# Seven block products for gate and up in layer 0 as in layer 1, activation forms summed by accumulating DMAs, and adaLN columns spread anew, in a two-layer trunk

## The chip, the cores and the metric

The kernel runs as one program on one core of a Trainium2 chip. The metric is the time of one execution on the device, in microseconds. TensorE does the matmuls, ScalarE (ACT) and VectorE (DVE) the elementwise work, GpSimd (POOL) some sums; SyncE (SP) and GpSimd issue the DMAs.

## The reference, cut to what matters

Two layers work on x of 512 tokens by 1024 channels, in float32. Each layer has a mixer and a gated MLP of inner width 2816. The adaLN parameters are six vectors of 1024 for each layer, from one conditioning vector. The change touches the MLP of layer 0, the forms of both MLPs, and the time at which adaLN columns are computed.

```python
def adaln_params(c, w, b):
    m = jax.nn.silu(c) @ w + b
    return [t[:, None, :] for t in jnp.split(m, 6, axis=-1)]

def conv_ffn(h, w_gate, w_up, conv_w, conv_b, w_down):
    a = causal_dwconv(h @ w_gate, conv_w, conv_b)
    return (jax.nn.silu(a) * (h @ w_up)) @ w_down

for layer in range(DEPTH):
    sh1, sc1, g1, sh2, sc2, g2 = adaln_params(c, ada_w[layer], ada_b[layer])
    h = rms_norm(x, norm_mix_g[layer]) * (1.0 + sc1) + sh1
    ...
    x = x + g1 * mix
    h = rms_norm(x, norm_ffn_g[layer]) * (1.0 + sc2) + sh2
    x = x + g2 * conv_ffn(h, ffn_w_gate[layer], ffn_w_up[layer], ffn_conv_w[layer],
                          ffn_conv_b[layer], ffn_w_down[layer])
```

## The kernel before, in words

Activations are kept transposed: 128 channels on the partitions, 512 tokens along the row, and 8 such chunks for 1024 channels. Every projection is a product of three matmuls (`mm3`, L209): each operand is split into a rounded high part and a remainder, and high by high, high by low and low by high are added up in PSUM. A weight unit is 128 x 1024 (512 KB). SyncE loads it, ScalarE writes its high part (`whi`, L169 or L200), VectorE the remainder (`wlo`, L170 or L201). The tokens form two halves of 256, LO and HI.

**The MLP in layer 0** (`ffn`, L705) takes the 22 blocks of 128 inner channels one after the other. For each, gate and up are 24 matmuls of 512 columns each. The blocks come in groups of 8, 7 and 7; after a group the down projection of that group runs for 8 output chunks m, and `add_x` (L324) adds each to x. The first two blocks are done by `ffn_start` (L690), half by half, while the norm of the other half is still being written. After each block `ada_step(3)` (L229) handles three adaLN columns: a load of 512 KB and one VectorE operation (L225). Behind the last down projection `tail` (L630) lets the next layer's norm begin, and `kv_start` (L1042) starts the K and V projections of layer 1; `prefetch` and `take` (L183, L188) prepare weights ahead in the order of `unit_order`.

**The MLP in layer 1** (`ffn_pairs`, L771) takes the first two blocks in the same way, and the other 20 as ten pairs. For a pair, gate and up together are a 2 x 2 product of blocks (gate and up by channels 0 to 511 and 512 to 1023, times LO and HI tokens), and seven products A to G take the place of eight (`product`, L906). Each product has 2 x 12 matmuls of 256 columns. Four of the products use sums of weights: s1 and s3 are added up by accumulating DMAs of GpSimd (L868), s2 and s4 by GpSimd's tensor operation (L873). Four use sums of activations, the forms n1, n2, t3 and t4: GpSimd first adds high and low parts (`whole`, L811), VectorE subtracts (`form`, L819 and L821), and ScalarE and VectorE split the result.

The order of a pair stage is set by the list `order`: product A of pair i, then B, C, D of pair i - 1, then E, F, G of pair i. After pairs 3 and 7 a down phase of 8 chunks is put in. `upkeep` (L1003) runs ahead of the list: it loads up to 9 entries ahead, starts up to 4 sums, and prepares up to 4 weights. Buffers come from rings: 3 for "raw" tiles, 4 for "sw" (sums and D's weight), 2 for "adaw" (s2 and s4), 4 for prepared weights.

## Time and profile before

| | before |
|---|---|
| time of three runs | 1144.04, 1148.44, 1151.24 us (median 1148.44) |
| the profiled execution | 1145.14 us |
| its span on the core | 1143.4 us |
| TensorE busy | 1112.9 us, 97% |
| VectorE busy | 834.5 us, 73% |
| ScalarE busy | 535.4 us, 47% |
| GpSimd busy | 111.2 us, 10% |

The span is the time from the first to the last instruction of the profiled execution; 1.7 us lie around it. "Busy" is the time in which an engine executes. TensorE's matmuls overlap one another, so its cost is read from the distance of their starts and not from their durations.

### The profile page before, as it was taken

How to read it: one execution, taken by the hardware profiler on the slowest of the kernel's cores; microseconds unless marked ns; L12 is line 12 of the kernel's file. 1: busy time of each engine (PE TensorE's matmuls, PEld its weight loads, DVE VectorE, ACT ScalarE, POOL GpSimd, SP SyncE). 2: the span in 40 equal slices, each digit the busy share in tenths (PEclk: the TensorE clock that was granted, in tenths of full speed). 3: DMA queues.
4: the chain of work that ended last, by engine and by line, in shares of the span. 5: the costliest groups of instructions: out<-in, count | busy, mean ns of one | idle time of the engine just before them, and what ended most of it. 6: DMA issues, size and time to landing. Idle time of an engine off the chain costs nothing.

```text
span 1143.4 us, 16343 instructions
## 1 busy us (share of the span) xinstructions
PE 1112.9 (97%) x6290; PEld 937.4 (82%) x6290; DVE 834.5 (73%) x1283; ACT 535.4 (47%) x864; POOL 111.2 (10%) x99
## 2 busy tenths in 40 slices
PE   8998998999999999999999999999899999999998
PEld 7866776798878888888889766678899889998997
DVE  6975899888873587456557578967999539974873
ACT  4465778354331333223335466644566326641550
POOL 0010000000000000000000111211633102411200
PEclk9999899999999999999999999999999999999999
DMA  9879573625874477445241421035358527573521
GB/s 341 297 188 234 179 213 121 199 69 168 274 225 143 135 225 236 160 148 164 81 143 57 111 57 55 19 93 143 80 136 222 158 77 198 135 236 92 132 72 74
DMA packets 49147, 174.03 MB, mean 152 GB/s; under 512 B 5583, under 2 KB 6735, under 8 KB 48367
## 3 DMA queue, kind: packets, MB, share of 16 engines
q1 hardware_dynamic: 44830, 156.64, 42.9%
q0 software_dynamic: 4240, 16.35, 7.8%
q8 instruction: 49, 0.80, 0.3%
q14 instruction: 28, 0.23, 0.1%
HBM read 164.06 MB, written 2.10 MB: 145 GB/s over the span
## 4 chain that ended last, share of the span: by engine, by line
PE 80%; DVE 9%; DMA 4%; ACT 3%; issue 2%; POOL 1%; SPq 0%; DVEq 0%; ACTq 0%; POOLq 0%
PE y L917 9%; PE d L212 7%; PE d L211 7%; PE d L210 7%; PE x L917 7%; DMA adaw<-adaw 4%; PE g L210 3%; PE g L212 3%; PE g L211 3%; PE u L212 3%; PE u L210 3%; PE u L211 3%; PE o L210 2%; PE o L212 2%; PE o L211 2%
## 5 line engine op out<-in xcount | busy, mean ns | idle before, releaser
L169 ACT ACTIVATE whi_w<-raw_w 128x1024 fp32r<-128x1024 f32 (+1 forms) x113 | 117.8, 1043 | 187.6 <-PE d L211 80.0
L170 DVE TENSOR_TENSOR wlo_w<-raw_w,whi_w 128x1024 fp32r<-128x1024 f32 (+1 forms) x113 | 135.9, 1203 | 46.0 <-ACT whi_w L169 43.5
L225 DVE CUSTOM_DVE_ANT_0 adaw<-adaw,c_s,col 128x1024 f32<-128x1024 f32 x80 | 101.3, 1279 | 35.1 <-DMA adaw<-adaw 34.9
L324 DVE SCALAR_TENSOR_TENSOR x<-d,ada,x 128x512 f32<-128x512 f32 (+1 forms) x51 | 36.6, 719 | 113.9 <-PE d L212 113.9
L211 PE MATMUL g<-h,whi_w 128*128 128x512 f32 (+1 forms) x192 | 72.2, 376 | 3.5 <-DVE h L301 3.5
L210 PE MATMUL g<-h,whi_w 128*128 128x512 f32 (+1 forms) x192 | 72.4, 377 | 1.6 <-ACT h L299 1.4
L212 PE MATMUL u<-h,wlo_w 128*128 128x512 f32 (+1 forms) x192 | 72.1, 376 | 0.0
L210 PE MATMUL d<-ah,whi_w 128*128 128x512 f32 (+1 forms) x190 | 71.9, 378 | 0.2 <-ACT ah L200 0.2
L210 PE MATMUL u<-h,whi_w 128*128 128x512 f32 (+1 forms) x192 | 72.0, 375 | 0.0
L212 PE MATMUL g<-h,wlo_w 128*128 128x512 f32 (+1 forms) x192 | 72.0, 375 | 0.0
L211 PE MATMUL d<-al,whi_w 128*128 128x512 f32 (+1 forms) x190 | 70.8, 373 | 0.8 <-DVE al L201 0.8
L211 PE MATMUL u<-h,whi_w 128*128 128x512 f32 (+1 forms) x192 | 71.5, 372 | 0.0
L212 PE MATMUL d<-ah,wlo_w 128*128 128x512 f32 (+1 forms) x190 | 71.3, 376 | 0.0
L873 POOL TENSOR_TENSOR r_s<-r_s,r_a 128x1024 f32<-128x1024 f32 x20 | 55.1, 2755 | 147.6 <-DVE wlo_s L201 50.2
L200 ACT ACTIVATE whi_s<-r_s 128x1024 fp32r<-128x1024 f32 x40 | 42.5, 1062 | 46.0 <-PE d L211 17.8
L212 PE MATMUL d<-ah,wlo_d 128*128 128x512 f32 (+1 forms) x158 | 60.8, 385 | 0.0
L210 PE MATMUL d<-ah,whi_d 128*128 128x512 f32 (+1 forms) x158 | 60.1, 380 | 0.6 <-DVE x L324 0.6
L211 PE MATMUL d<-al,whi_d 128*128 128x512 f32 (+1 forms) x158 | 60.5, 383 | 0.0
L917 PE MATMUL y<-h,whi_a 128*128 128x256 f32 x320 | 57.1, 280 | 1.0 <-DVE gt L789 1.0
L1121 POOL COPY sc<-nsink 128x4 f32<-128x4 f32 x16 | 3.4, 217 | 560.9 <-PE d L212 502.3
L917 PE MATMUL y<-forms,whi_s 128*128 128x256 f32 x320 | 56.6, 279 | 0.1
L201 DVE TENSOR_TENSOR wlo_s<-r_s,whi_s 128x1024 fp32r<-128x1024 f32 x40 | 51.9, 1297 | 5.6 <-ACT whi_s L200 4.7
(332 smaller groups left out, 3119.8 us busy)
## 6 DMA issues: line engine op xcount, KB each, us to landing
raw_w<-wu SPq DMA_DIRECT2D x104, 512.0 KB, 3.8
adaw<-adaw SPq DMA_DIRECT2D x80, 512.0 KB, 4.4
r_a<-ws SPq DMA_DIRECT2D x30, 512.0 KB, 3.8
r_s<-ws SPq DMA_DIRECT2D x20, 512.0 KB, 4.6
r_s<-ws POOLq DMA_DIRECT2D x20, 512.0 KB, 7.2
first_w<-adaw SPq DMA_DIRECT2D x16, 512.0 KB, 5.7
r_d<-wu SPq DMA_DIRECT2D x16, 512.0 KB, 5.2
raw_w<-w SPq DMA_DIRECT2D x16, 448.0 KB, 3.4
```

The source lines that it names most:

```text
L169: pin(A.activation(hi[:, :n], raw[:, :n], AF.Copy))
L170: pin(V.tensor_tensor(out=lo[:, :n], in0=raw[:, :n], in1=hi[:, :n].bitcast(F32), op=ALU.subtract))
L200: A.activation(dst_hi, src, AF.Copy)
L201: V.tensor_tensor(out=dst_lo, in0=src, in1=dst_hi.bitcast(F32), op=ALU.subtract)
L210: PE.matmul(out, whi, rhi, start=first, stop=False)
L211: PE.matmul(out, whi, rlo, start=False, stop=False)
L212: return PE.matmul(out, wlo, rhi, start=False, stop=last)
L225: return V.tensor_tensor_reduce(out=t, in0=t, in1=c_s, scale=1.0, scalar=C(f"ada_b{l}", s * 8 + m), op0=ALU.mult, op1=ALU.add, accum_out=a ...
L324: V.scalar_tensor_tensor(out=x[:, m, sl], in0=bank[:, sl], scalar=ada_ap(l, s, m), in1=x[:, m, sl], op0=ALU.mult, op1=ALU.add)
L873: G.tensor_tensor(out=self.t, in0=self.base[0].t, in1=self.base[1].t, op=ALU.add)
L917: m = [PE.matmul(out, w[a][:, o:o + P], b[c][:, k], start=slot in "AEF" and k + a + c == 0, stop=k == 3 and a == 1, skip_group_check=True) ...
L1121: nc.gpsimd.tensor_copy(sc[:, :, 256:257], nsink[:, 4 * kv:4 * kv + 4].unsqueeze(2))
```

## The change

One function `ffn` now serves both layers, and both take gate and up of the ten pairs as seven block products. In layer 0 this puts 1680 matmuls of 256 columns in the place of 960 of 512 columns. The groups of 8, 7 and 7 are gone; the down projection runs after pairs 3 and 7 and in pieces at the end, as layer 1 did.

The forms of both layers are made in another way. While a norm's chunk is written, ScalarE writes a second output from the same input (`extra`): b11 and n21 in the LO half, n12 and b22 in the HI half, which are whole activations with a plus or a minus. GpSimd then adds them by accumulating DMAs from SBUF to SBUF (`add_to`), of 256 KB each, and ScalarE and VectorE split the sums. The tensor operations L811, L819 and L821 are gone.

The adaLN columns become entries of the list `order` (`ada_item`) and load into the ring "sw", which grows from 4 to 6 buffers. In layer 0 one stands in each of the stages 2 to 9, two ahead of each of the 16 down blocks, and two near the end. 53 columns are left when the MLP of layer 0 begins, before and after the change; 42 are now handled in it, 3 at the end of layer 1's attention, and 8 around the first down phase of layer 1.

The rest of the lists: `upkeep` looks 12 entries ahead for loads instead of 9; the activations of the inner blocks have 8 buffers for each of the two names instead of 10; at the end of layer 0 the weights of V and of the last two down blocks are prepared, then `prefetch(1)` prepares one more, and `tail` begins. The gate weights of the recurrence move to a tile with two buffers.

```diff
+        nrm.forms = b = b_forms(l)
+        def extra(m, sl, t):
+            if m < 4:
+                A.activation(b["b11"][:, m], t[:, sl], AF.Identity, bias=ada_ap(l, 3, m))
+            else:
+                A.activation(b["n21"][:, m - 4], t[:, sl], AF.Identity, bias=nsh[:, l, m:m + 1], scale=-1.0)
+        nrm.extra = extra
         for u in range(2):
...
+    def ffn(l, nrm, nxt=None, before=None, after=None):
         LO, HI = HALVES
...
+            early = [bank(n == "u", f"{n}{l}_{i}") for i in range(2) for n in ("g", "u")]
+            units = [unit(f"{n}{l}", i) for i in range(2) for n in ("g", "u")]
+            pairs = [(b, take(u, 2 - j, pin)) for j, (b, u) in enumerate(zip(early, units))]
+            proj2(pairs, LO)
+            b11, n21 = (nrm.forms[n] for n in ("b11", "n21"))
+            n12, b22 = act_tiles(f"n12_{l}", (P, 2, 256), F32), act_tiles(f"b22_{l}", (P, 2, 256), F32)
+            def extra(m, sl, t):
+                if m < 4:
+                    A.activation(n12[m // 2][:, m % 2], t[:, sl], AF.Identity, bias=nsh[:, l, m:m + 1], scale=-1.0)
+                else:
+                    A.activation(b22[m // 2 - 2][:, m % 2], t[:, sl], AF.Identity, bias=ada_ap(l, 3, m))
+            nrm.extra = extra
+            nrm.start(HI)
+            nrm.half(HI)
+            rings = {"raw": (3, []), "sw": (6, []), "adaw": (2, []), "w": (4, [])}
...
+            def add_to(a, b):
+                for i in range(2):
+                    G.dma_start(a[i], b[i], accum_op=ALU.add)
+            def split_form(dst, src, neg=False):
+                for i in range(2):
+                    hi, lo = (d[:, 2 * i:2 * i + 2] for d in dst)
+                    A.activation(hi, src[i], AF.Copy, scale=-1.0 if neg else 1.0)
+                    if neg:
+                        V.scalar_tensor_tensor(out=lo, in0=src[i], scalar=-1.0, in1=hi.bitcast(F32), op0=ALU.mult, op1=ALU.subtract)
+                    else:
+                        V.tensor_tensor(out=lo, in0=src[i], in1=hi.bitcast(F32), op=ALU.subtract)
+            def twos(t):
+                return [t[:, 2 * i:2 * i + 2] for i in range(2)]
+            fb, fn = twos(b11), twos(n21)
+            def first_form():
+                add_to(fb, n12)
+                split_form(n1, fb)
+            def other_forms():
+                b, n = fb, fn
+                add_to(b, b22)
+                split_form(n2, b, True)
+                add_to(b22, n12)
+                add_to(b, n)
+                split_form(t3, b22)
+                split_form(t4, b)
             st = [{} for _ in range(NST)]
...
             def slot(i, n):
                 order.append((blocks[i][n], lambda w: product(i, n), True))
 
-            tails = [Item(f"dt{i}", ws[4 * NST + i], "raw") for i in range(3)]
+            def ada_item():
+                if ada_q:
+                    q = ada_q.pop(0)
+                    order.append((Item("ada_%d_%d_%d" % q, adaw[q[0], q[1] * 8 + q[2]], "sw", ada=q), None, True))
+            tails = [Item(f"dt{l}_{i}", ws[l * NWS + 4 * NST + i], "raw") for i in range(3)]
             for i in range(NST):
                 slot(i, "A")
                 if i:
                     for n in "BCD":
                         slot(i - 1, n)
+                if l == 0 and i > 1:
+                    ada_item()
                 for n in "EFG":
                     slot(i, n)
                 if i in DOWN_AFTER:
                     gi = DOWN_AFTER.index(i)
                     for m in range(KC):
-                        order.append((Item(f"d{gi}_{m}", wu[UNITS["d1"] + 8 * gi + m], "raw"),
+                        ada_item()
+                        ada_item()
+                        order.append((Item(f"d{l}_{gi}_{m}", wu[UNITS[f"d{l}"] + 8 * gi + m], "raw"),
                                       lambda w, gi=gi, m=m: down(gi, m, w), True))
             order.append((tails[0], lambda w: down_part(0, w), False))
             slot(NST - 1, "B")
@@ -996,13 +972,17 @@
             slot(NST - 1, "C")
             slot(NST - 1, "D")
             order.append((tails[1], lambda w: (down_part(2, w), down_part(3, w)), True))
+            ada_item()
+            ada_item()
             order.append((tails[2], down_rest, True))
...
+            def upkeep(c, sums=4):
+                for it, _, _ in order[c:c + 12]:
                     if it.t is None and it.base is None:
                         if not it.room():
...
+            rings["w"][1].extend(Held() for _ in range(2))
+            upkeep(0, 2)
+            first_form()
+            for i in ((0, 1), (2, 3)):
+                proj2([pairs[j] for j in i], HI)
+            n2, t3 = (pair_of(t) for t in kept(f"forms{l}", [P, 2, 4, 256]))
+            forms = {"A": p11, "B": t3, "C": p22, "D": t4, "E": p21, "F": n1, "G": n2}
+            other_forms()
+            for held in rings["w"][1][:2]:
+                held.left = 0
+            for f in range(2):
+                finish(f, early[2 * f], early[2 * f + 1], 1.0)()
+            for c, (it, run, done) in enumerate(order):
                 upkeep(c)
+                if it.ada is not None:
+                    with tc.high_priority(offset=-100):
+                        pin(ada_col(*it.ada, it.t))
+                    it.left = 0
+                    continue
...
+                return None
+            pending.extend(unit_order(1))
+            prep_spare([unit("l1_v", u) for u in range(2)], kept("spare1", [P, 2, 1024]))
+            for it in last[2:]:
+                it.prep()
+            prefetch(1)
+            tail(nxt, lambda m, sl, mid=None: down_last(m, last[m - 4].w, (sl,), mid), (KC - 2, KC - 1), before)
+            return after()
 
```

What this does to the order of the instructions is seen at three places.

ScalarE, second half of the norm at the start of layer 0's MLP: `h` are the high parts that gate and up of the first two blocks wait for, `ahn` and `aln` are n12, `ahb` and `alb` b22, `b` is b11, `n` is n1. Before:

```order
L299 ACTIVATE h_0_1880<-ht_1_3_256_2280,ada 128x256 [waits DVE_49]
L299 ACTIVATE h_0_1880<-ht_1_4_256_2284,ada 128x256 [waits DVE_49]
L299 ACTIVATE h_0_1880<-ht_1_5_256_2288,ada 128x256 [waits DVE_49]
L299 ACTIVATE h_0_1880<-ht_1_6_256_2292,ada 128x256 [waits DVE_49]
L299 ACTIVATE h_0_1880<-ht_1_7_256_2296,ada 128x256 [waits DVE_49]
L169 ACTIVATE whi_w_2448<-raw_w_2446 128x1024 [waits DMAHW6_49,PE_49]
```

After:

```order
L296 ACTIVATE h_0_1880<-ht_1_4_256_2301,ada 128x256 [waits DVE_49]
L748 ACTIVATE ahb_0_2271<-ht_1_4_256_2301,ada 128x256
L296 ACTIVATE h_0_1880<-ht_1_5_256_2306,ada 128x256 [waits DVE_49]
L748 ACTIVATE ahb_0_2271<-ht_1_5_256_2306,ada 128x256
L841 ACTIVATE n_0_2321<-b_0_1886 128x512 [waits DMASW5_49,Activation_49]
L296 ACTIVATE h_0_1880<-ht_1_6_256_2311,ada 128x256 [waits DVE_49]
L748 ACTIVATE alb_0_2272<-ht_1_6_256_2311,ada 128x256
L296 ACTIVATE h_0_1880<-ht_1_7_256_2316,ada 128x256 [waits DVE_49]
L748 ACTIVATE alb_0_2272<-ht_1_7_256_2316,ada 128x256
L841 ACTIVATE n_0_2321<-b_0_1886 128x512 [waits DMASW6_49,Activation_49]
```

The extra outputs stand between the high parts, and the first split of n1 stands ahead of the chunks 6 and 7 with a wait for an accumulating DMA.

VectorE, end of a down phase (`x<-d` are the last output chunks, `wlo` the remainders of the weights of the next products). Before, in layer 1:

```order
L324 SCALAR_TENSOR_TENSOR x<-d_0_5_7964,ada,x 128x512 [waits PE_49]
L201 TENSOR_TENSOR wlo_s_3_7991<-r_s_3_7888,whi_s_3_7990 128x1024 [waits DMASW6_49,Activation_49]
L324 SCALAR_TENSOR_TENSOR x<-d_0_6_7994,ada,x 128x512 [waits PE_49]
L201 TENSOR_TENSOR wlo_s_3_8023<-r_s_3_7650,whi_s_3_8022 128x1024 [waits Activation_49]
L324 SCALAR_TENSOR_TENSOR x<-d_0_7_8026,ada,x 128x512 [waits PE_49]
L201 TENSOR_TENSOR wlo_a_3_8055<-r_a_3_7890,whi_a_3_8054 128x1024 [waits Activation_49]
L201 TENSOR_TENSOR wlo_a_4_8089<-r_a_4_7923,whi_a_4_8088 128x1024 [waits DMAHW6_49,PE_49,Activation_49]
```

After, in layer 0, the same place:

```order
L322 SCALAR_TENSOR_TENSOR x<-d_0_5_3592,ada,x 128x512 [waits PE_49]
L322 SCALAR_TENSOR_TENSOR x<-d_0_6_3633,ada,x 128x512 [waits PE_49]
L197 TENSOR_TENSOR wlo_s_0_3_3619<-r_s_0_3_3586,whi_s_0_3_3618 128x1024 [waits DMASW2_49,Activation_49]
L197 TENSOR_TENSOR wlo_s_0_3_3662<-r_s_0_3_3248,whi_s_0_3_3661 128x1024 [waits Activation_49]
L221 ISA r_ada_0_1_3510,ada<-r_ada_0_1_3510,c_s,col 128x1024 [waits DMAHW4_49]
L221 ISA ada 128x1
L221 ISA r_ada_0_2_3513,ada<-r_ada_0_2_3513,c_s,col 128x1024 [waits DMAHW5_49]
L221 ISA ada 128x1
L221 ISA r_ada_0_3_3548,ada<-r_ada_0_3_3548,c_s,col 128x1024 [waits DMAHW7_49]
L221 ISA ada 128x1
L322 SCALAR_TENSOR_TENSOR x<-d_0_7_3669,ada,x 128x512 [waits PE_49]
L197 TENSOR_TENSOR wlo_a_0_3_3698<-r_a_0_3_3590,whi_a_0_3_3697 128x1024 [waits DMAHW2_49,Activation_49]
```

The adaLN columns (L221) now stand between the last chunks and the remainders.

TensorE, the first matmuls of K and V for layer 1 behind the down projection (`k_0`, `k_1` are K's two banks, `v_0` a bank of V, `h_0` and `h_1` high and low parts of the norm). Before:

```order
L210 MATMUL k_0_4871<-h_0_1880,whi_w_4689 128x256 [waits Activation_49]
L211 MATMUL k_0_4871<-h_1_1881,whi_w_4689 128x256 [waits DVE_49]
L212 MATMUL k_0_4871<-h_0_1880,wlo_w_4690 128x256
L210 MATMUL k_1_4872<-h_0_1880,whi_w_4721 128x256
L211 MATMUL k_1_4872<-h_1_1881,whi_w_4721 128x256
L212 MATMUL k_1_4872<-h_0_1880,wlo_w_4722 128x256
L210 MATMUL k_0_4871<-h_0_1880,whi_w_4689 128x256 [waits Activation_49]
L211 MATMUL k_0_4871<-h_1_1881,whi_w_4689 128x256 [waits DVE_49]
L212 MATMUL k_0_4871<-h_0_1880,wlo_w_4690 128x256
L210 MATMUL k_1_4872<-h_0_1880,whi_w_4721 128x256
```

After, from the sixth chunk of the same half on:

```order
L206 MATMUL k_0_5930<-h_0_1880,whi_5792 128x256 [waits Activation_49]
L207 MATMUL k_0_5930<-h_1_1881,whi_5792 128x256 [waits DVE_49]
L208 MATMUL k_0_5930<-h_0_1880,wlo_5793 128x256
L206 MATMUL k_0_5930<-h_0_1880,whi_5792 128x256 [waits Activation_49]
L207 MATMUL k_0_5930<-h_1_1881,whi_5792 128x256 [waits DVE_49]
L208 MATMUL k_0_5930<-h_0_1880,wlo_5793 128x256
L272 MATMUL ms_0_256_6044<-ones,acc_0_1879 128x1 [waits DVE_49]
L272 MATMUL ms_0_256_6044<-ones,acc_0_1879 128x1
L206 MATMUL k_1_5931<-h_0_1880,whi_5938 128x256 [waits Activation_49]
L207 MATMUL k_1_5931<-h_1_1881,whi_5938 128x256
L206 MATMUL v_0_5932<-spare_0_5768,h_0_1880 128x256
```

Before, the products of `k_1` are interleaved with those of `k_0`; after, they follow behind the whole half of `k_0`, with a wait for ScalarE, and `ms` of the other half's norm stands ahead of them.

## Rows read from the trace of the kernel before

**Rows 1.** The page: the busy times, the chain's shares by engine
```profile
PE 1112.9 (97%) x6290; PEld 937.4 (82%) x6290; DVE 834.5 (73%) x1283; ACT 535.4 (47%) x864; POOL 111.2 (10%) x99
...
PE 80%; DVE 9%; DMA 4%; ACT 3%; issue 2%; POOL 1%; SPq 0%; DVEq 0%; ACTq 0%; POOLq 0%
```

**Rows 2.** Windows: stretch and length, then busy time by engine, granted clock, DMA share, GB/s
```profile
241.80:608.70 366.90, 365.87 (x1738) 305.77 (x1739) 239.88 (x336) 125.49 (x166) 0.00 (x0) 1.00 0.53 168
608.70:632.40 23.70, 23.70 (x203) 23.62 (x201) 19.76 (x42) 11.83 (x22) 0.33 (x2) 1.00 0.23 67
800.00:840.00 40.00, 34.60 (x254) 33.15 (x254) 38.18 (x50) 21.88 (x36) 23.50 (x12) 0.91 0.41 98
836.00:838.00 2.00, 2.00 (x12) 2.00 (x10) 2.00 (x4) 0.52 (x2) 0.38 (x1) 0.51 0.77 203
860.00:880.00 20.00, 20.00 (x172) 20.00 (x172) 19.38 (x22) 12.57 (x18) 6.75 (x4) 1.00 0.71 187
901.00:938.00 37.00, 37.00 (x163) 30.36 (x162) 15.52 (x14) 7.44 (x7) 3.99 (x2) 1.00 0.30 95
962.00:982.00 20.00, 20.00 (x179) 20.00 (x178) 18.88 (x22) 13.11 (x19) 6.50 (x4) 1.00 0.65 171
```

**Rows 3.** The chain (start, us, what): direct matmuls in layer 0, products in layer 1
```profile
265.59 0.23 PE g L210
...
377.06 0.23 PE g L210
...
388.04 0.23 PE g L210
...
861.76 2.83 PE x L917 x24
...
966.84 2.72 PE y L917 x24
```

**Rows 4.** Waits of TensorE, 785 to 842 us: us in total, times, longest
```profile
PE g L211 <- DVE h L301: 3.5, 4, 1.6
...
PE y L917 <- DVE gt L789: 1.0, 1, 1.0
PE y L917 <- DVE wlo_a L201: 1.0, 1, 1.0
```

**Rows 5.** Timeline of VectorE: start, us, line, operation, tiles, count, idle time before
```profile
613.96 0.89 DVE L301 SCALAR_TENSOR_TENSOR h<-ht,ada,h 128x256 fp32r<-128x256 f32 x2 [0.19 <-ACT h L299]
...
801.61 3.53 DVE L301 SCALAR_TENSOR_TENSOR h<-ht,ada,h 128x256 fp32r<-128x256 f32 x2 [0.18 <-ACT h L299]
...
960.25 3.84 DVE L201 TENSOR_TENSOR wlo_a<-r_a,whi_a 128x1024 fp32r<-128x1024 f32 x2
...
965.18 1.22 DVE L201 TENSOR_TENSOR wlo_s<-r_s,whi_s 128x1024 fp32r<-128x1024 f32 x1 [0.42 <-ACT whi_s L200]
```

**Rows 6.** The page, DMA issues: KB each, median us from issue to landing
```profile
adaw<-adaw SPq DMA_DIRECT2D x80, 512.0 KB, 4.4
...
r_s<-ws POOLq DMA_DIRECT2D x20, 512.0 KB, 7.2
...
k<-k POOLq DMA_DIRECT2D x4, 256.0 KB, 4.7
```

**Rows 7.** The page, costliest groups: the adaLN operation
```profile
L225 DVE CUSTOM_DVE_ANT_0 adaw<-adaw,c_s,col 128x1024 f32<-128x1024 f32 x80 | 101.3, 1279 | 35.1 <-DMA adaw<-adaw 34.9
```

**Rows 8.** Groups of VectorE and GpSimd at the forms of layer 1
```profile
L819 DVE SCALAR_TENSOR_TENSOR r<-r,r 128x512 f32<-128x512 f32 x4 | 4.8, 1230 | 0.0
L821 DVE TENSOR_TENSOR r<-r,r 128x512 f32<-128x512 f32 x4 | 3.2, 813 | 1.1 <-POOL r L811 1.1
...
L811 POOL TENSOR_TENSOR r<-h,h 128x512 f32<-128x512 f32 x8 | 12.1, 1527 | 39.1 <-DVE h L301 39.1
```

**Rows 9.** Waits of TensorE, 80 to 135 us
```profile
PE gr L210 <- ACT ge L529: 4.1, 1, 4.1
PE pr L210 <- ACT xcs L200: 2.2, 1, 2.2
```

More of the change, by code (lines that the diff above doesn't have):

```diff
@@ L792, in finish @@
                 return close
-            def pair_of(t):
-                return [t[:, i] for i in range(2)]
-            n1 = pair_of(pool.tile([P, 2, 4, 256], F32R, tag="n1", name="n1", bufs=1))
-            n2, t3 = (pair_of(t) for t in kept("forms", [P, 2, 4, 256]))
-            half = [slice(0, 4), slice(4, 8)]
-            b11, b21 = ([h[:, k, LO] for h in (hh, hl)] for k in half)
-            b22 = [h[:, half[1], HI] for h in (hh, hl)]
-            t4 = [h[:, half[0], HI] for h in (hh, hl)]
@@ L888, in ffn_pairs, with __init__ @@
             class Held:
-                def __init__(self, item):
-                    item.held, self.left = self, 1
+                def __init__(self, item=None):
+                    self.left = 1
+                    if item is not None:
+                        item.held = self
             blocks = []
             for i in range(NST):
-                b = [ws[4 * i + j] for j in range(4)]
-                a11, a12 = Item(f"a11_{i}", b[0], "raw"), Item(f"a12_{i}", b[1], "raw")
-                a22 = Item(f"a22_{i}", b[3], "sw")
@@ L899, in ffn_pairs @@
[L899 to L903 removed]
+                b = [ws[l * NWS + 4 * i + j] for j in range(4)]
+                a11, a12 = Item(f"a11_{l}_{i}", b[0], "raw"), Item(f"a12_{l}_{i}", b[1], "raw")
```

285 lines of the change are left out of this document (97 added, 188 removed).

## The prediction

> **What bounds the kernel now.** The page comes first: TensorE is busy for 97% of the span and holds 80% of the chain of waits, the next engine is VectorE with 73% [rows 1]. So time can only go if TensorE gets less to do, or less to wait for, and each edit is priced by what TensorE issues and by what it is made to wait for. Then the windows, stage by stage. Layer 0's MLP lasts 366.9 us, TensorE idles for 1.0 us of them, VectorE works 239.9 (65%), GpSimd not at all [rows 2]: this stage is bound by matmuls alone. In layer 1 the stages of pairs look different: TensorE is full there too, but VectorE works 18.9 to 19.4 us of every 20 [rows 2]. The one place in layer 1's MLP where TensorE waits is its beginning: of the 40 us from 800 on it is busy for 34.6, at a granted clock of 0.91 [rows 2], and its waits name VectorE: 3.5 us for the norm's second half, 1.0 for a weight's remainder, 1.0 for the first inner block [rows 4].
>
> **The change part by part.** All sums are made against the profiled execution of 1145.1 us; the median of the runs is 1148.4, 3.3 above it, and the change in us is then taken from the median.
>
> *The products.* A direct matmul of 512 columns costs TensorE (388.04 - 377.06)/48 = 0.229 us [rows 3]; 960 of them are 219.6 us. The products have two prices in layer 1: 2.83 us for 24 before the first down phase, 2.72 behind it [rows 3]. Four stages of seven slots at the first and six at the second are 79.2 + 114.2 = 193.5. That is **-26.1**. If the higher price held in all ten stages, it would be 4.6 less. The down projection keeps its 528 matmuls' worth of columns and is taken at the same price. The 1.0 us of waiting [rows 2] is replaced by what follows: **-1.0**.
>
> *The beginning of layer 0's MLP.* Now the 192 matmuls of the first two blocks run from 241.8 to 265.6, 23.8 us [rows 2, 3]. In the new order ScalarE meets the first split of n1 ahead of the last two chunks, and this waits for an accumulating DMA from SBUF to SBUF of 256 KB. No such DMA is in the trace. The nearest are GpSimd's plain ones of that size, 4.7 us, and its accumulating ones of twice the size, 7.2 [rows 6]. The last two chunks come some five chunks behind the output that the DMA adds; at about 1 us for a chunk, and near 1 us for the issue (my estimate, from the 6 us that the eight chunks at the start of K and V take, below), the wait is between 0.7 and 3.2, and with the added outputs on ScalarE I take 2.7. TensorE needs these chunks at once, so nothing hides it. Next, t4 stands at the end of a chain of three such additions, 14.1 to 21.6 us from the first. VectorE has t4's split ahead of the remainder for A of the second pair; from the first addition TensorE has about 4 us of the second half and four products of 2.83 to do, 15.3 us of cover. The wait is then 0 to 6.3; I take 2.2, nearer to the plain DMA since the size is its size. The two waits of layer 1 that follow on a VectorE that is behind, 1.0 and 1.0 [rows 4], I take over: 2.0. Together **+6.9**, between 1 and 13.
>
> By the Trainium skill (DMA: Bandwidth & Descriptors, the section on the anatomy of one DMA on the GpSimd path) a DMA costs about 2.0 us plus its bytes at 436 GB/s, 2.6 us for 256 KB, an estimate from its figures; the row of that size shows 4.7. By the page's figure the waits for both splits would go and the sum would be about 4 us lower.
>
> *adaLN columns in the stages.* One is 1.28 us on VectorE [rows 7] and a read of 0.08. A stage of 19.04 us holds 18.88/20 of VectorE's time, 18.0 us, in the undisturbed window [rows 2]; with a column it is 19.3, over by 0.3. That is 2.4 us over eight stages, if nothing else gives way; VectorE's small idle pieces say less, a column meeting a sum on GpSimd says more: two remainders took 3.84 us there where one alone takes 1.22 [rows 5], so 1.4 us for one encounter. At the two passages from a down phase to the next stage, three columns (4.1 us) stand on VectorE between the last chunks' residuals and the remainders for D and A, as the order shows; one column each is taken to show on TensorE, 2.6 us. Sum **+5.0**, between 0 and 14. In the down phases themselves 16 columns are 21.8 us, beside 15.52/37 x 44 = 18.5 of work [rows 2], 40.3 of 44 us: covered, by little. Their loads raise 95 GB/s by 16 x 0.52 MB in 44 us, 191, to 286 GB/s; the row's 0.30 for 95 GB/s makes that a share of 0.90 [rows 2]. Covered too, but a load can be late, and SyncE issues the columns' loads ahead of weights; a cost is left to a rival. The eight columns in layer 1's down phase find 21 idle us [rows 2], and the three at the end of its attention lie beside the output projection: 0 for both, at most 4.1 for the latter.
>
> *The start of K and V.* In the trace TensorE is full from 608.7 to 632.4 [rows 2], because two weights of K and a part of V feed on every chunk that comes. The last of the eight chunks is done at 614.85 [rows 5]. In these 6.15 us it does 52 matmuls of 0.118 (2.83/24). With only k_0 at hand it can do 24; the other 28 are late: 3.3 us. k_1's high part stands behind the last chunk on ScalarE, its remainder on VectorE; half a remainder, 0.6, is added. And a TensorE that is fed in pieces is granted a lower clock: after two waits of 1.0 [rows 4] the window from 836 to 838 shows 0.51, the lower level of 1.2 GHz, and 12 matmuls where 17 belong [rows 2]; 0.7 for that. **+4.6**, between 3 and 8.
>
> *The forms in layer 1.* VectorE loses 4.8 + 3.2 us of subtractions, and GpSimd 12.1 us of sums [rows 8]. What VectorE then has left over goes into the 2.0 us of waits behind the second half [rows 4] and the 1 us that the low clock cost [rows 2]: all but 1 us of the 3. The 3.5 us in the second half [rows 4] I leave, since in the new order the split of n1 waits in that place, and n12's DMAs stand behind two weight sums and two weight DMAs on GpSimd. **-2.0**, between -6 and +2.
>
> What was slow about the old forms shows in one row: two operations of the norm took 3.53 us on VectorE while GpSimd added [rows 5], the same pair at the start of K and V 0.89. The Trainium skill (SBUF — State Buffer, the section on who interferes with whom) has a rule for this: a VectorE instruction with two inputs from SBUF contends with a GpSimd instruction that reads SBUF, and a DMA contends with no compute engine. By it the 3.5 us go too; the same rule speaks against layer 0, which gets 20 more sums of weights on GpSimd.
>
> *The recurrence.* The gates' weights and loads move a little; TensorE waits there for 4.1 and 2.2 us [rows 9], for ScalarE, whose order changes only in two splits. Zero, between -2 and +2.
>
> Sum: -26.1 - 1.0 + 6.9 + 5.0 + 4.6 - 2.0 = **-12.6**: 1132.5 for the profiled execution, 1135.8 for the median, **1136**.
>
> **The rivals.**
>
> *The gain arrives nearly whole.* The additions land in time and VectorE keeps up. For it speaks that VectorE has 35% of layer 0's MLP free [rows 2]. The Trainium skill's rule on contention (SBUF — State Buffer, above) speaks for it in layer 1 as well. Left are -27.1, the late 28 matmuls (+3.3), and -5 in layer 1: -28.8, 1120.
>
> *Layer 0 becomes bound by VectorE and the loads.* VectorE has 0.3 us too much in every stage with a column, and the queues run at 0.90 in the down phases, so that a late weight stops TensorE. The upper ends hold: +14 for the +5.0, and 3 more at the beginning: -0.6, 1148, no change. Against it: the ring of prepared weights is four deep, and the stages of layer 1 at 18.9 of 20 show no wait on TensorE.
>
> *Slower than before.* One mechanism: the chain of additions. My 2.2 us for t4 stand for (15.3 + 2.2)/3 = 5.8 us an addition. Each further us costs three in each layer, six in all. At 8.0 us nothing is left of the gain; at 10, which a queue shared with weight DMAs of 7.2 [rows 6] could give, it is 1136 + 25 = 1161.
>
> That the products stay at 2.83 in all of layer 0 gives 1140; it lies inside the forecast's own range.
>
> **How the numbers follow.** The forecast, 1127 to 1142, gets 0.45; the whole gain (1115 to 1127) 0.22; the bound layer 0 (1142 to 1154) 0.27; the chain 0.06. A measurement of this kernel can tell about 1%, 11.5 us, from no change: faster is under 1137, slower over 1160. Some three quarters of the forecast lie under 1137 with the whole gain: 0.56 faster, 0.38 the same, 0.06 slower. The range leaves out a third of the whole gain at the bottom, and the chain and the upper end of the third case at the top: 1118 to 1150.
>
> **What would show it.** The products: some 193 us between the first A and the last D of layer 0, without the down blocks, and 24 in 2.72 to 2.83. The beginning: the wide part starts 26 to 27 us behind the first matmul, and the largest waits name the split of n1 and a remainder. The columns: VectorE over 18.5 of 19 us in stages 4 to 9, and waits of TensorE for remainders behind the down phases. K and V: 24 matmuls in the first 6 us, and a granted clock under 1. Layer 1: waits of 3 to 4 us in the second half, and no low clock behind it. The prediction fails if the additions land much earlier or later than 5.8 us, or if VectorE's overload adds up over the stages.

## The result and the profile after

The changed kernel takes 1178.42 us (median of four runs, 1175.28 to 1180.48), the kernel before 1147.56 beside it (1144.04 to 1151.24). The ratio is 1.0266 with a 95% interval from 1.0226 to 1.0307: slower by 2.7%, about 31 us. The forecast was 1136 with a range up to 1150; the result lies outside it, on the other side.

The profiled execution after took 1175.28 us with a span of 1173.5, 30.1 more than before. The page's busy times answer to [rows 1]:

```profile
PE 1106.1 (94%) x7004; PEld 967.9 (82%) x7004; DVE 905.2 (77%) x1374; ACT 596.7 (51%) x973; POOL 174.8 (15%) x147
```

TensorE's busy time fell by 6.8 us, its idle time rose from 30.5 to 67.4. So less work was bought with more waiting. Where it waits is found by cutting the span at five starts of TensorE that both traces have: the first gate matmul of layer 0's MLP, the first K matmul behind it, the first gate matmul of layer 1's MLP, the first pair product of layer 1, and the last matmul, which starts 3.9 and 3.8 us ahead of the span's end.

| stretch | before, us | after, us | difference | forecast |
|---|---|---|---|---|
| up to layer 0's MLP (the recurrence) | 241.8 | 245.8 | +4.0 | 0 |
| layer 0's MLP | 367.0 | 376.7 | +9.7 | -15.2 |
| K, V and the attention of layer 1 | 180.9 | 185.0 | +4.1 | +4.6 |
| start of layer 1's MLP, to its first product | 30.9 | 39.6 | +8.7 | 0 |
| the rest, to the last matmul | 318.9 | 322.6 | +3.7 | -2.0 |

The -2.0 of the forecast stands in the last row because the two waits that it counts on, for `gt` and `wlo_a` [rows 4], lie behind layer 1's first product, which starts at 820.6 us in the kernel before. Two places hold most of the miss: layer 0's MLP, 25 us worse than forecast, and the start of layer 1's MLP, 8.7 worse. The windows of the trace after show both (stretch and length, then busy time of TensorE, its weight loads, VectorE, ScalarE and GpSimd, granted clock, DMA share, GB/s; they answer to [rows 2]):

```profile
245.80:622.50 376.70, 353.67 (x2453) 330.37 (x2453) 312.76 (x407) 177.09 (x256) 74.28 (x48) 0.96 0.69 200
260.00:280.00 20.00, 17.18 (x123) 16.97 (x124) 15.63 (x20) 10.39 (x19) 11.82 (x11) 0.83 0.98 210
345.00:392.00 47.00, 47.00 (x224) 39.28 (x224) 34.23 (x50) 10.51 (x12) 0.88 (x1) 1.00 0.76 246
392.70:433.50 40.80, 32.46 (x241) 31.59 (x240) 32.13 (x39) 16.54 (x23) 13.67 (x8) 0.87 0.77 207
409.40:416.50 7.10, 5.35 (x24) 5.05 (x25) 7.05 (x7) 3.95 (x5) 5.46 (x3) 0.52 0.47 107
440.00:460.00 20.00, 20.00 (x172) 20.00 (x171) 19.96 (x24) 12.59 (x18) 6.76 (x4) 1.00 0.70 208
528.50:569.10 40.60, 32.57 (x241) 31.80 (x240) 32.70 (x40) 16.54 (x23) 13.72 (x8) 0.87 0.73 209
622.50:628.70 6.20, 4.34 (x21) 2.73 (x19) 5.65 (x15) 2.98 (x8) 0.32 (x2) 1.00 0.00 0
807.50:847.10 39.60, 27.70 (x201) 26.52 (x202) 23.14 (x40) 17.93 (x39) 15.08 (x13) 0.87 0.83 206
```

Read these against each other. In a stage of pairs (440 to 460) VectorE has no time left, 19.96 of 20, and TensorE is full all the same. In the first down phase (348.8 to 392.7; the window is 345 to 392) TensorE is full too, and the DMA share is 0.76. But each passage from a down phase to the next stage (392.7 to 433.5 and 528.5 to 569.1) holds ten products, which at the paces of [rows 3] are 27.2 to 28.3 us, and takes 40.7. This is where layer 0 lost its gain: 25 to 27 us in two places, at a granted clock of 0.87.

What TensorE waits for in the first passage (waits of TensorE, 385 to 435 us: total, times, longest):

```profile
PE y L878 <- DVE x L893: 3.9, 1, 3.9
PE x L878 <- ACT whi_s L196: 2.6, 1, 2.6
PE x L878 <- DVE wlo_s L197: 1.7, 1, 1.7
```

`whi_s` and `wlo_s` are the split sums of weights. The waits make 8.2 us of the 12.5 to 13.6; the rest goes with the low clock that follows on them: the 24 matmuls of the window from 409.4 to 416.5 take 5.35 us at a granted clock of 0.52, near the lower level of 1.2 GHz, in place of 2.83. ScalarE's row says what the split waited for, and the timeline of SyncE's queue says why that came late (start, us, line, operation, tiles):

```profile
408.32 1.06 ACT L196 ACTIVATE whi_s<-r_s 128x1024 fp32r<-128x1024 f32 x1 [11.45 <-DMA r_s<-ws]
```

```profile
373.07 0.33 SPq L781 DMA_DIRECT2D r_a<-ws  x1
374.28 1.54 SPq L781 DMA_DIRECT2D r_ada<-adaw  x2
379.77 0.33 SPq L781 DMA_DIRECT2D r_s<-ws  x1
380.98 0.33 SPq L781 DMA_DIRECT2D r_a<-ws  x1
391.84 0.33 SPq L781 DMA_DIRECT2D r_ada<-adaw  x1
394.18 1.53 SPq L781 DMA_DIRECT2D r_s<-ws  x2
396.59 0.33 SPq L781 DMA_DIRECT2D r_a<-ws  x1
```

`r_s` are the weights that the next stage adds up, `r_ada` the adaLN columns. From 318 to 375 SyncE issued 16 columns and not one `r_s`; between 380.98 and 391.84 it issued nothing at all; and the weights of the sum for the product that was due at 406.8 were loaded at 394, with the addition still to come (it landed at 408.2). Columns and sums share the ring "sw". The longest wait, for `x`, is VectorE's: it came to that operation late, behind a remainder of 2.79 us that ran beside another late sum on GpSimd.

At the start of layer 1's MLP GpSimd stands in the way, and ScalarE behind it (timelines of the two engines):

```profile
810.42 1.84 POOL L789 DMA_DIRECT2D r_s<-ws  x2 [38.12 <-DVE ht L292]
819.48 5.03 POOL L794 TENSOR_TENSOR r_s<-r_s,r_a 128x1024 f32<-128x1024 f32 x2 [7.22 <-DVE ht L292]
824.47 1.74 POOL L789 DMA_DIRECT2D r_s<-ws  x2
825.59 1.51 POOL L836 DMA_DIRECT2D b<-ahn  x1
```

```profile
826.40 0.51 ACT L296 ACTIVATE h<-ht,ada 128x256 fp32r<-128x256 f32 x1
826.81 0.49 ACT L748 ACTIVATE ahb<-ht,ada 128x256 f32<-128x256 f32 x1
836.75 0.63 ACT L841 ACTIVATE n<-b 128x512 fp32r<-128x512 f32 x1 [9.44 <-DMA b<-ahn]
837.29 0.49 ACT L296 ACTIVATE h<-ht,ada 128x256 fp32r<-128x256 f32 x1
```

The addition `b<-ahn` (n12 into b11) is issued behind two sums and four accumulating weight DMAs and lands 11.1 us later; ScalarE's split of n1 waits 9.44 us for it, and the chunk of the norm that TensorE needs (`h` at 837.29) stands behind the split. TensorE's wait for that chunk is the 9.3 here (waits of TensorE, 807 to 847.2 us):

```profile
PE g L206 <- ACT h L296: 10.7, 2, 9.3
```

### The profile page after: what moved, and what is told of

It reads as the page before. It is cut to its first block, busy times and chain, and to the rows that moved or that the text cites. A ratio compares the mean times of both kernels' runs of the same rounds, so it can differ in the third digit from the quotient of the medians.

```text
span 1173.5 us, 18262 instructions
## 1 busy us (share of the span) xinstructions
PE 1106.1 (94%) x7004; PEld 967.9 (82%) x7004; DVE 905.2 (77%) x1374; ACT 596.7 (51%) x973; POOL 174.8 (15%) x147
## 3 DMA queue, kind: packets, MB, share of 16 engines
q0 software_dynamic: 9424, 31.04, 14.5%
## 5 line engine op out<-in xcount | busy, mean ns | idle before, releaser
L878 PE MATMUL y<-forms,whi_s 128*128 128x256 f32 x640 | 118.1, 285 | 13.0 <-DVE x L893 8.6
L207 PE MATMUL d<-al,whi_d 128*128 128x512 f32 (+1 forms) x322 | 122.4, 380 | 0.0
L208 PE MATMUL d<-ah,wlo_d 128*128 128x512 f32 (+1 forms) x322 | 121.8, 378 | 0.0
L206 PE MATMUL d<-ah,whi_d 128*128 128x512 f32 (+1 forms) x322 | 121.7, 378 | 0.0
L878 PEld LDWEIGHTS y<-forms,whi_s 128*128 128x128 f32 x640 | 100.6, 193 | 14.3 <-issue 9.3
L197 DVE TENSOR_TENSOR wlo_a<-r_a,whi_a 128x1024 fp32r<-128x1024 f32 x60 | 99.0, 1660 | 13.9 <-ACT whi_a L196 13.2
L878 PEld LDWEIGHTS y<-h,whi_a 128*128 128x128 f32 x640 | 98.4, 189 | 1.4 <-issue 1.1
L789 POOL DMA_DIRECT2D r_s<-ws x40 | 35.5, 919 | 423.8 <-DVE ht L292 180.9
L196 ACT ACTIVATE whi_a<-r_a 128x1024 fp32r<-128x1024 f32 x60 | 63.6, 1060 | 63.0 <-PE y L878 33.9
L878 PE MATMUL y<-forms,wlo_s 128*128 128x256 f32 x320 | 91.0, 285 | 0.0
L878 PE MATMUL y<-h,wlo_a 128*128 128x256 f32 x320 | 89.6, 280 | 0.3 <-DVE wlo_a L197 0.3
L196 ACT ACTIVATE whi_d<-r_d 128x1024 fp32r<-128x1024 f32 (+1 forms) x40 | 40.7, 1018 | 90.7 <-PE d L207 77.0
L165 ACT ACTIVATE whi<-raw 128x1024 fp32r<-128x1024 f32 x49 | 51.7, 1057 | 46.2 <-PE o L207 23.8
L207 PEld LDWEIGHTS d<-al,whi_d 128*128 128x128 f32 x322 | 60.5, 188 | 11.5
```

The costliest lines, as they stand in the source:

```text
L165: pin(A.activation(hi, raw, AF.Copy))
L196: A.activation(dst_hi, src, AF.Copy)
L197: V.tensor_tensor(out=dst_lo, in0=src, in1=dst_hi.bitcast(F32), op=ALU.subtract)
L206: PE.matmul(out, whi, rhi, start=first, stop=False)
L207: PE.matmul(out, whi, rlo, start=False, stop=False)
L208: return PE.matmul(out, wlo, rhi, start=False, stop=last)
```

## The experiments

All ratios are to the kernel before on the same chip, with 95% intervals. Each diff is against the changed kernel unless it says otherwise.

**Columns left out of layer 0's MLP.** The 42 columns are neither loaded nor computed there.

```diff
+            if l == 0:
+                V.tensor_copy(ada[:, 0, 43:48], ada[:, 0, 0:5])
+                V.tensor_copy(ada[:, 1, 0:40], ada[:, 0, 0:40])
             def ada_item():
-                if ada_q:
+                if l == 0:
+                    if len(ada_q) > 11:
+                        ada_q.pop(0)
+                elif ada_q:
```

> The changed kernel without the 42 adaLN columns that layer 0's MLP now carries (they are left out; their places are filled by a copy of other columns, so the output is another one). Theory: the two passages from a down phase to the next pair stage lose 27 us together because sums of weights are loaded behind these columns; without the columns both passages are as smooth as in layer 1 before, 1178 - 25 = 1153. Rival, VectorE overloaded in layer 0's stages by its own work beside the sums on GpSimd: the waits stay but for the columns' 1.3 us each, 1178 - 8 = 1170.

1157.74 us, ratio 1.0059 [1.0026, 1.0092], against 1.0266 for the change. Layer 0's MLP falls from 376.7 to 357.8 us. Both passages are gone: ten products take 28.3 us, the pace of 2.83, and TensorE waits nowhere between the first products and K. The first passage of this kernel:

```profile
402.50:430.80 28.30, 28.30 (x242) 28.30 (x241) 22.82 (x28) 16.92 (x23) 6.52 (x4) 1.00 0.53 147
```

The columns cause the loss in the passages; what of them does is left to the next two kernels.

**A ring of their own for the columns.** All columns stay (diff shortened); two of the six buffers of "sw" become a ring "adac", and the look-ahead counts weights alone and goes on past a column that has no buffer.

```diff
-            rings = {"raw": (3, []), "sw": (6, []), "adaw": (2, []), "w": (4, [])}
+            rings = {"raw": (3, []), "sw": (4, []), "adac": (2, []), "adaw": (2, []), "w": (4, [])}
...
-                    order.append((Item("ada_%d_%d_%d" % q, adaw[q[0], q[1] * 8 + q[2]], "sw", ada=q), None, True))
+                    order.append((Item("ada_%d_%d_%d" % q, adaw[q[0], q[1] * 8 + q[2]], "adac", ada=q), None, True))
...
-                for it, _, _ in order[c:c + 12]:
+                n = 0
+                for it, _, _ in order[c:]:
+                    if it.ada is None:
+                        n += 1
+                        if n > 9:
+                            break
                     if it.t is None and it.base is None:
                         if not it.room():
+                            if it.ada is not None:
+                                continue
                             break
```

> The same columns on VectorE, but their loads have a ring of two buffers of their own (the sums' ring goes back to four), do not count in the look-ahead (nine entries of weights) and never hold back the weights behind them. Theory (late loads of the sums): 1178 - 20 = 1158 or less, and the waits of 2 to 4 us behind the down phases gone. Rival (VectorE's time for the columns, or its contention with GpSimd's sums): nothing of that changes, 1175 to 1180.

1156.63 us, 1.0062 [1.0037, 1.0088]: as good as leaving the columns out. The two passages are 29.1 and 30.4 us long in place of 40.8 and 40.6. So it is neither VectorE's time for the columns nor the bytes that they load, since both are as in the change.

**The ring alone,** with the look-ahead of the change (of the diff above, the lines on the ring and the tile's tag only). I held that the look-ahead, which stops at an entry without a buffer, was the cause; the rival was the buffers themselves.

> A ring of two buffers of their own for the adaLN columns (sums' ring four), but the look-ahead counts them as before and stops where their ring is full. Theory that the columns hold back the weights by standing among them in the list: the waits behind the down phases stay, 1170 to 1180. Rival, that they took the sums' buffers: 1157, as with the full cure.

1157.91 us, 1.0085 [1.0054, 1.0115]. My theory fell: passages of 30.2 and 31.0 us without touching the look-ahead. The first passage, then SyncE's queue and GpSimd in this kernel:

```profile
397.60:427.80 30.20, 28.39 (x241) 28.05 (x240) 28.73 (x35) 16.85 (x23) 9.16 (x5) 1.00 0.65 186
```

```profile
336.02 0.33 SPq L781 DMA_DIRECT2D r_s<-ws  x1
...
341.16 0.33 SPq L781 DMA_DIRECT2D r_s<-ws  x1
...
349.19 0.33 SPq L781 DMA_DIRECT2D r_ada<-adaw  x1
350.96 7.58 SPq L781 DMA_DIRECT2D r_d<-wu  x3
```

```profile
342.46 0.88 POOL L789 DMA_DIRECT2D r_s<-ws  x1 [4.21 <-DMA r_d<-wu]
346.42 0.86 POOL L789 DMA_DIRECT2D r_s<-ws  x1 [3.08 <-DMA r_s<-ws]
```

The weights of the sums are now loaded and their additions issued ahead of the beginning of the down phase (351.7), the loads 54 to 58 us earlier than the same two at 394 and 395 in the change. Layer 0's MLP is 362.2 us: 14.5 less than after the change, though the passages give 20.2; the other 5.7 went into down phases of 45.9 and 44.5 us instead of 44.0 (2.4), into longer fourth and fifth products (1.5) and into the slower pace told of at the end.

The change itself has a counterpart in layer 1. There 8 columns stand ahead of the first 4 blocks of the first down phase, in the same ring of six; the weights of the sums are loaded at 930.7 to 942.8, in the first half of that phase (921.6 to 965.6), and the passage behind it takes 28.3 us for ten products. So the shared ring alone costs nothing; columns that hold it up to the end of the down phase do.

**The gates' weights in one buffer,** as before, though under another tag (before they were two tiles of their own).

```diff
-            gw = work.tile([P, 2, 256], F32R, tag="sq", name=f"gw{c}")
+            gw = work.tile([P, 2, 256], F32R, tag="acc", name=f"gw{c}", bufs=1)
```

> The changed kernel with a single buffer for the recurrence's gate weights, as before. Theory: the 4.0 us by which layer 0's MLP begins later come from the order of the splits on ScalarE there; 1178 - 4 = 1174, and the wait of pr falls from 5.8 back to about 2.2. Rival, the loads of that stretch: no change, 1178.

1176.0 us, 1.0237 [1.0201, 1.0273]: the interval overlaps that of the change, so the whole time doesn't decide it. The stretch does. The 32 matmuls of the recurrence's gate projection, first and last start (before, after, this kernel):

```profile
L210 PE MATMUL gr<-h,whi_w x32: 388/394/796, 84.1 to 132.0; 128*128 128x512 f32 x32
```

```profile
L206 PE MATMUL gr<-h,whi x32: 388/394/796, 84.1 to 135.8; 128*128 128x512 f32 x32
```

```profile
L206 PE MATMUL gr<-h,whi x32: 388/393/792, 86.9 to 135.0; 128*128 128x512 f32 x32
```

They take 47.9, 51.7 and 48.1 us. The wait for ScalarE of the product `pr`, which is interleaved with it, 2.2 us before [rows 9], is 5.8 after and 2.4 here. The other kernels of this section bear it out: first to last matmul of the projection takes 47.8 to 49.1 us in those with one buffer and 52.1 to 52.9 in those with two. The new tile costs some 3.6 us in this stretch. The time up to layer 0's MLP shows it only over several kernels, 242.6 to 246.0 us with one buffer and 245.8 to 250.0 with two: it is 246.0 here against 245.8 after the change, because the projection began 2.8 us later, in a part of the kernel that the edit doesn't touch.

**The additions of n12 first.** In both layers GpSimd issues the accumulating DMAs of two sums, then the additions of n12, and then the first tensor sums; `pin` holds that order (diff shortened).

```diff
-            upkeep(0, 2)
-            first_form()
+            upkeep(0, 1)
+            blocks[0]["B"].sum()
+            add_to(fb, n12)
+            upkeep(0, 2)
+            hold[0] = False
+            split_form(n1, fb)
```

> At the beginning of both MLPs GpSimd issues the additions of n12 ahead of its first two sums of weights (the order on GpSimd is held there). Theory: the 9.3 us wait of layer 1 came from the additions standing behind two sums and two weight DMAs, and the norm's remainders were held by the same sums: 1178 - 12 = 1166, the wait under 3 us. Rival, the additions land late because the queue is full of weight DMAs, wherever they stand: 1178 - 3 = 1175, landing still 9 us and more.

1173.63 us, 1.0205 [1.0163, 1.0246]. This interval too overlaps that of the change; the stretches decide. The 9.3 us are gone, and layer 1's start is back to 30.9 us as before: the first addition is issued 13.3 us behind the first gate matmul in place of 18.1, and lands in 8.0 us in place of 11.1. Two remainders of the norm still take 2.89 and 2.01 us beside the sums, so these are not what the 9.3 us were. Waits of TensorE from 812 to 870 us:

```profile
PE y L883 <- ACT p L892: 4.0, 1, 4.0
PE g L207 <- DVE h L298: 2.9, 2, 2.3
PE g L206 <- ACT h L296: 1.6, 2, 1.4
```

Layer 0's MLP, however, grew by 4.0 to 380.7. Its first product comes 0.8 us later, and the fourth to sixth take 2.0 us more, since the sums that now come later are late for G and A: TensorE waits 3.0 us for a remainder of a sum that it did not wait for in the change. The rest goes with the slower pace told of at the end. The order that helps in layer 1 doesn't help in layer 0, where the split had not waited for the first addition.

**Old forms,** by GpSimd's sums and VectorE's subtractions as before, in both layers; against the kernel with the columns' own ring (shortened):

```diff
-            first_form()
...
-            other_forms()
+            r11, r12 = whole("r11", 0, LO), whole("r12", 0, HI)
+            form(n1, r11, r11, r12, False)
+            r22, r21 = whole("r22", 1, HI), whole("r21", 1, LO)
+            form(n2, r11, r11, r22, True)
+            form(t3, r12, r22, r12, False)
+            form(t4, r11, r11, r21, True)
```

> With the columns' own ring and look-ahead (1156.6), both MLPs make their forms as before: sums on GpSimd, subtractions on VectorE, no accumulating DMAs of activations. Theory that the new forms cost time: from the first matmul of gate to the first product 31 us in both layers (layer 1 now 36.3, layer 0 30.6), the waits for p and the split of t4 gone: 1156.6 - 8 = 1149. Rival, the old forms' contention costs as much in layer 0 as it saves: 1156.

1152.5 us, 1.0030 [1.0002, 1.0057], against 1.0062 for the same kernel with accumulating DMAs; the intervals overlap. Layer 1's start is 31.7 instead of 36.3 us, layer 0's MLP 359.0 instead of 358.1. As the change orders them, the DMAs make the forms no cheaper in either layer.

**Two of K's weights ahead,** against the kernel with the columns' own ring: `prefetch(2)` in the place of `prefetch(1)`.

> With the columns' own ring (1156.6), two weights instead of one are prepared ahead of the tail of layer 0, so that both halves of K are at hand. Theory: the 28 late matmuls come back, 1156.6 - 4.6 = 1152, and no waits of K's first matmuls. Rival, the stretch up to layer 1's MLP is set by what comes behind K and V: no change, 1156.6.

1151.12 us, 0.9997 [0.9961, 1.0033]. From the first K matmul to layer 1's MLP it is 182.2 us instead of 186.9, and TensorE waits for nothing at the start of K. The missing weight cost 4.7 us, against 4.6 in the forecast.

**All of it:** own ring, `prefetch(2)`, the old gates' tile, and n12 first in layer 1 alone.

> The columns' own ring, two weights ahead of the tail, the gate weights with one buffer, and in layer 1 the additions of n12 ahead of the first sums of weights. If the terms add: 1156.6 - 4.6 - 2.4 - 5.5 = 1144, just under the kernel before. Rival, the terms hide one another: 1150.

1142.5 us, 0.9936 [0.9911, 0.9962]: faster than the kernel before by 0.6%, the first here in which the products' gain reaches the end. Its page and the window of layer 0's MLP:

```profile
PE 1095.6 (96%) x7004; PEld 957.4 (84%) x7004; DVE 912.0 (80%) x1374; ACT 598.7 (53%) x973; POOL 178.1 (16%) x147
```

```profile
242.60:601.20 358.60, 348.02 (x2452) 324.35 (x2453) 312.67 (x408) 179.77 (x257) 76.64 (x48) 0.99 0.72 211
```

**All of it with the old forms.**

> The last cure (own ring, two weights ahead of the tail, one buffer for the gate weights: 1142.5 with the additions of layer 1 moved) with the forms made as before in both layers. Theory, that the accumulating DMAs gain nothing once they are issued early: 1142 to 1146. Rival, that they are worth what the form change was for (VectorE's 8 us of subtractions and GpSimd's 12 us of sums in each layer): 1150 or more.

1143.58 us, 0.9954 [0.9925, 0.9984]. The interval overlaps the one with DMAs: once both are ordered well, no difference between the two ways of making forms can be measured.

**All of it, with layer 0's sums behind the additions.** Against the kernel with all of it; in layer 0 the first two tensor sums follow the additions of n12 and b22, so that none runs beside the norm's remainders (diff shortened).

```diff
-            else:
-                upkeep(0, 2)
-                add_to(fb, n12)
+                hold[0] = False
...
                 add_to(b, b22)
+                upkeep(0, 2)
+                hold[0] = False
                 split_form(n2, b, True)
```

> The same cure with the new forms, and in layer 0 too the first two sums of weights stand behind the additions of n12 and b22. Theory, that GpSimd's two sums held the norm's remainders on VectorE (waits of 1.0 and 2.2 us and a slow clock behind them): from the first matmul of gate to the first product 26 us instead of 29.8, 1142.5 - 3 = 1139. Rival, that the sums then come too late for products G and C: no gain, 1143.

1146.53 us, 0.9969 [0.9943, 0.9995]. The start of layer 0's MLP to the first product is 27.2 instead of 29.8 us, but TensorE then waits 2.0 us for the remainder of a sum and 3.5 for a VectorE that is late, neither of which it does in the kernel with all of it, and the whole MLP is 361.8 instead of 358.6 us. What the norm gains the products give back.

## Why the prediction was wrong, point by point

**The products: right.** Outside the passages and the first five a product of 24 matmuls starts every 2.72 to 2.83 us in layer 0, but for three of 3.51, 2.92 and 2.91. These are the two prices that the -26.1 was made of, though the higher one stands between the down phases and not ahead of the first. The gain exists; it was spent elsewhere.

**The adaLN columns: the step that failed.** The forecast gave 2.4 us to the stages, 2.6 to the passages and nothing to the down phases ("Covered too, but a load can be late"). The stages cost next to nothing: VectorE is at 19.96 of 20 and TensorE at 20.00, and the three longer products make 1.0 us. The down phases cost nothing: they last 44.0 us, as the 44 of the forecast's own sum. But the passages cost 25 to 27 us. I looked for what the columns take from VectorE and from the queues, and they took buffers. A column holds a place in "sw" from its load until VectorE has used it, and with two columns ahead of every down block they filled the ring, so that the sums of the next stage could be loaded neither ahead of the down phase, as with rings apart, nor during it. That the ring is the cause is shown by the kernel that changes the ring alone. With rings apart the passages cost 1.9 + 2.7 us over ten products at the pace of 2.83 there, and the down phases 2.4 more: 7.0, against the +5.0 of the forecast for the whole of the columns. The diff had the ring and its six places in plain sight; the rival "bound by VectorE and the loads" named late weights, but priced them by bytes and let them cost 14 at most.

**The beginning of layer 0's MLP: size too small, and its largest part from another cause.** To the first product it is 30.4 us after against 23.8 before [rows 2], +6.6, and the fourth and fifth product take 5.0 and 4.05, +3.6 over the 2.72 of their neighbours: 10.2, against +6.9 and a range up to 13 (the forecast's own upper terms, 3.2, 6.3 and 2.0, make 11.5). The 2.7 that the forecast gave to the first split of n1, for its wait for the addition ahead of the last two chunks, did not come: the split starts without idle time on ScalarE. What held TensorE is VectorE beside GpSimd (timelines of ScalarE, of VectorE, then of GpSimd):

```profile
266.16 0.61 ACT L841 ACTIVATE n<-b 128x512 fp32r<-128x512 f32 x1
```

```profile
258.50 2.07 DVE L298 SCALAR_TENSOR_TENSOR h<-ht,ada,h 128x256 fp32r<-128x256 f32 x1
...
261.06 2.68 DVE L298 SCALAR_TENSOR_TENSOR h<-ht,ada,h 128x256 fp32r<-128x256 f32 x1
...
264.25 0.48 DVE L298 SCALAR_TENSOR_TENSOR h<-ht,ada,h 128x256 fp32r<-128x256 f32 x1
```

```profile
257.78 2.50 POOL L794 TENSOR_TENSOR r_s<-r_s,r_a 128x1024 f32<-128x1024 f32 x1 [7.29 <-DMA r_a<-ws]
...
260.81 2.65 POOL L794 TENSOR_TENSOR r_s<-r_s,r_a 128x1024 f32<-128x1024 f32 x1
```

A remainder of the norm takes 0.48 us alone and 2.07 and 2.68 while a sum of weights runs on GpSimd; TensorE waits 3.3 us for them and 1.4 for a high part behind them, and then runs at the clock of 0.83 that the window from 260 to 280 shows. The Trainium skill (SBUF — State Buffer, Who interferes with whom) says that a VectorE instruction with two inputs from SBUF contends with a GpSimd instruction that reads SBUF. The trace agrees: each long remainder ends 0.3 us behind the sum beside it, and with the sums moved behind the additions all remainders take 0.48. The forecast had weighed this rule for layer 1 and named it against layer 0, without putting a price on it there.

The forecast's own wait does exist, but shows only where the contention is gone, in the kernel with layer 0's sums behind the additions (timeline of ScalarE):

```profile
263.18 0.63 ACT L846 ACTIVATE n<-b 128x512 fp32r<-128x512 f32 x1 [2.46 <-DMA b<-ahn]
```

ScalarE waits 2.46 us there, near the 2.7, and the 27.2 us to the first product are 3.4 above the 23.8 before.

The +3.6 of the two products stand against 4.2 in the forecast (2.2 for t4, 2.0 for a VectorE that is behind). The longest wait there is 2.0 us for `p`, the copy of a product that ScalarE makes behind the splits of t4, and not for a remainder on VectorE. The first two additions landed in 5.8 and 5.9 us, the 5.8 that the forecast had worked out, but this is in part luck: the eight of layer 0 took 3.4 to 7.1, and the chain ended 25.7 us behind its first issue, where the forecast had 15.3 + 2.2 = 17.5.

**K and V: right.** +4.1 in the result and 4.7 undone by one more weight, against 4.6. The +4.1 is at the low end: this stretch is 185.0 us after, 186.8 to 189.5 in the six other kernels with one weight ahead, and 180.8 to 182.2 in the four with two. Between 622.5 and 628.7 TensorE has 21 matmuls, where 55 stand in the same stretch before. The part of 0.7 that I gave to a low clock was wrong: the granted clock is 1.00 in that window.

**The forms in layer 1: wrong in sign.** -2.0 was forecast, for waits behind the first product, and nothing of it came: the two long products there take 9.85 us after and 9.93 before, with a wait of 2.4 us for ScalarE's `p` in the place of the two on VectorE. Ahead of the first product, where the forecast let the time stand, +8.7 came. The forecast saw that "n12's DMAs stand behind two weight sums and two weight DMAs on GpSimd" and still gave that the price of the 3.5 us of [rows 4]; issued late behind them, the additions took 11.1 and 11.8 us to land. With the additions ahead of the sums the loss is gone while the remainders still run long beside the sums, which shows that the place on GpSimd is the cause. Two further additions of the same size landed in 3.3 us in the same stretch, so the 11 us are not the operation's own. This was the forecast's slower rival, the chain of additions, in a simpler form: not three additions of 8 us each but the first, once.

The Trainium skill's figures (DMA: Bandwidth & Descriptors, the anatomy of one DMA on the GpSimd path) gave an estimate of 2.6 us for such an addition. No run agrees: between 3.3 and 11.8 us were measured, and the measurement decides. (Without the waits for both splits the forecast would have been 2.7 + 2.2 = 4.9 us lower, not about 4.)

**The recurrence: missed.** 0 was forecast, with 2 either way, and +4.0 came. The tile of the gates' weights, which I passed over as a small move, accounts for some 3.6 of it: 3.5 is also the difference between the mean starts of layer 0's MLP in the kernels with one and with two buffers.

**The rest of layer 1: not shown to be the change's.** +3.7, the pace of the products, told below.

Summed up: the forecast was -12.6 and the span gave +30.1, 42.7 apart. Of these, 20 to 22 are the columns' term, 8.7 the start of layer 1, 2.0 the gain behind it that did not come, 4.0 the recurrence, 3.3 the start of layer 0, and 3.7 the rest of layer 1; the small ones nearly cancel. With the ring, the order on GpSimd, the gates' tile and K's weight put right the kernel is 7.3 us faster than before (1142.5 against 1149.81): layer 0's MLP then gains 8.4 us of the 15.2. Its start accounts for 4.0 of the rest (29.8 us to the first product, then products of 5.7 and 4.6), and the 28 products between the down phases, at 2.83 and not 2.72, for 3.0.

## What to carry to other kernels

When work is moved into a list that prefetches, ask first which buffers its loads hold and for how long, and who else loads into that ring; time on an engine and bytes on a queue can both be free and the ring still starve the stage that follows. Look at the slack phases (here the down projections) as the time by whose end the next stage's buffers must be filled, not as idle time to fill: columns in the first half of one cost nothing here, columns up to its end cost 12 to 14 us. And a DMA that a compute engine waits for in order should be issued ahead of long operations on its issuing engine, if what then stands behind it can wait (in layer 0 it could not).

## What the runs showed of the hardware that was not expected

The pair products run at one of two paces, 2.72 or 2.83 us for 24 matmuls of 256 columns, each held over long stretches (2.83 for some 250 us of layer 1 after) at a granted clock of 1.00. Before, layer 1 goes from 2.83 to 2.72 behind its first down phase [rows 3]; after, it stays at 2.83. The chains, after and then the kernel with `prefetch(2)` and the columns' own ring:

```profile
918.96 2.83 PE y L878 x24
...
965.73 5.65 PE y L878 x48
```

```profile
897.96 2.83 PE y L878 x24
...
944.75 5.44 PE y L878 x48
```

In both no wait stands at the change or at its absence. The last stretch of the table is 317.7 to 319.9 us in the kernels that change to 2.72 there, and 322.3 to 324.9 in those that don't, whatever their edit: the 45 products behind the first down phase, at 0.107 us each, are 4.8. Which pace a kernel takes was not found. The executions of one kernel spread as widely (without the columns 1148.0 to 1162.3 us), which would fit a pace that changes from execution to execution, but one execution of each kernel was profiled and this is not shown. The pace shifts comparisons by 4 us in layer 1, and can do so in layer 0 (the kernel without the columns runs 65 of its 70 products there at 2.83, the change less than half), more than several of the edits are worth. It is why the experiments are read by stretches and not by the whole time alone.
